# Differential attention scores: two rounded passes over split keys and queries in place of one zero-padded float32 product

## Chip, cores and metric

The kernel runs on one core of a Trainium2 chip. The metric is the device time of one execution in microseconds (us), as the median of the runs shown.

## The reference

Two layers of a trunk over 256 context and 256 latent tokens of width 1024. Three groups of heads work on the same normalised input, side by side: differential attention (group A), latent-compressed attention (group B, "MLA" in the code) and a recurrent scan (group C). A projection, and then a gated feed-forward part, follow. The change touches group A alone: four heads, each with two maps of scores of 64 dimensions.

```python
def diff_attn(q1, q2, k1, k2, v, lam):
    scale = A_DIM ** -0.5
    p1 = softmax32(jnp.einsum('bqhd,bkhd->bhqk', q1, k1) * scale)
    p2 = softmax32(jnp.einsum('bqhd,bkhd->bhqk', q2, k2) * scale)
    a = (p1 - lam * p2).astype(v.dtype)
    return jnp.einsum('bhqk,bkhe->bqhe', a, v)
```

Context queries see the 256 context keys, latent queries all 512. Latent queries and keys are turned by a rotary embedding first. Layer 0 needs both streams, layer 1 the latent queries alone, but the keys of both.

## The kernel before

Every tile has 128 partitions. Queries and keys are held with features on partitions and tokens along the free dimension, so one head's two maps fill the 128 rows: map 1 in rows 0 to 63, map 2 in rows 64 to 127.

Large products run as three rounded passes (`mm3`, L275 to L277): both operands are split into a rounded part and the rest, in the type `F32R` (`fp32r` in the rows), and high x high, high x low and low x high are summed in PSUM. `wgroup` splits each weight tile, rounding on ScalarE (L267) and subtracting on VectorE (L268).

The score product of the differential heads does not use this. `diff_project` makes a head's projection into a PSUM bank of the pool `g`, which has two; `diff_keys` and `diff_query` call it. Its context half is copied by ScalarE (L1070), its latent half goes through `rope` on VectorE (a shuffle at L874, two products, a sum at L882). The query is written twice, into the halves of a tile `qz` that GpSimd has filled with zeros elsewhere (`diff_queries`, L1059 and L1060): one half has map 1's rows and zeros under them, the other the reverse. With this one float32 product over all 128 rows at L1096 gives one map's scores, for 128 queries and 256 or 512 keys. Each product is two records in the trace.

What follows a score: VectorE takes the maximum of each row (L887, in `expsm`), ScalarE the exponential (L888), VectorE combines both maps (L1102), TensorE transposes (L895) and multiplies with the values (L899, in `pv`), ScalarE copies between these.

The work is written as a plan, a string of letters: `q2` projects keys and queries of head 2, `c2` and `l2` are that head's context and latent scores, `x` and `y` MLA heads, `a` a piece of the modulation's projection (L320), `s` steps of the recurrent scan, `v` the values. A scheduler then sets each engine's own order at build time, so instructions of several steps interleave, and engines run their rows strictly in that order. The recurrent part's triangular solver (L688, L690 on VectorE) runs beside the heads.

In layer 0 the weight loads of the output projection wait for the first score product of the last latent head (`late`, passed to `then`).

## Time and profile before

| | us |
|---|---|
| median of 3 runs | 1380.76 (1376.9 to 1381.56) |
| profiled execution | 1380.92 |
| its span | 1379.1 |
| TensorE busy in the span | 1316.6 |
| VectorE busy | 969.1 |
| ScalarE busy | 703.4 |

The span runs from the first to the last instruction. A matmul's record ends when its result is out, so records of successive matmuls overlap, and the step from start to start is what one costs in a row of them. The attention of layer 0 lies at some 240 to 375 us, that of layer 1 at 1037 to 1150.

### The profile page before, as it was taken

The numbers are of one execution on the slowest core, as the hardware profiler recorded it, in microseconds if no ns is written. First come the engines' busy times: TensorE is split into PE (matmuls) and PEld (weight loads), VectorE is DVE, ScalarE is ACT, GpSimd is POOL, SyncE is SP. The second block draws the span as 40 slices with busy tenths as digits, with TensorE's granted clock in tenths as the row PEclk, the third lists the DMA queues.
The fourth block names the chain that finished last, engine by engine and source line by source line (L and its number), as shares of the span: only waits on it lengthen the run. The fifth ranks groups of instructions, "written<-read, shape, count | busy, mean of one in ns | idle before, by whom it ended". The sixth has DMA issues, their size and how long they took to land.

```text
span 1379.1 us, 25815 instructions
## 1 busy us (share of the span) xinstructions
PE 1316.6 (95%) x10184; PEld 1058.2 (77%) x10184; DVE 969.1 (70%) x2430; ACT 703.4 (51%) x1375; POOL 21.1 (2%) x41
## 2 busy tenths in 40 slices
PE   6999999999899999999999999999998998899997
PEld 2687756476666888999998878889874765899996
DVE  3546756685784768866667689668769677867776
ACT  4425343666655454543445654646634654555543
POOL 0001000000000000000000000000100000000000
PEclk9999999999889999999999999999999999999998
DMA  9921342501566747433367436447220029866622
GB/s 317 272 66 47 108 142 95 178 1 62 184 201 211 220 147 232 152 108 107 92 194 262 138 126 196 136 133 222 77 62 1 2 83 315 230 184 187 188 78 84
DMA packets 213162, 201.38 MB, mean 146 GB/s; under 512 B 6528, under 2 KB 168832, under 8 KB 213040
## 3 DMA queue, kind: packets, MB, share of 16 engines
q1 hardware_dynamic: 213040, 199.72, 46.7%
q8 instruction: 80, 1.31, 0.4%
q14 instruction: 42, 0.34, 0.1%
HBM read 197.57 MB, written 2.13 MB: 145 GB/s over the span
## 4 chain that ended last, share of the span: by engine, by line
PE 80%; DVE 12%; ACT 3%; DMA 3%; issue 2%; SPq 0%; DVEq 0%; ACTq 0%
PE g L275 11%; PE g L276 10%; PE g L277 10%; PE acc L275 6%; PE acc L277 6%; PE acc L276 6%; PE r L275 3%; PE r L276 3%; PE r L277 3%; PE acc L320 2%; PE acc L899 2%; PE g L1096 2%; DMA wrm<-in_w_in_dram 1%; PE acc L895 1%; PE g L320 1%
## 5 line engine op out<-in xcount | busy, mean ns | idle before, releaser
L268 DVE TENSOR_TENSOR wlf<-wrf,whf 128x1024 fp32r<-128x1024 f32 x176 | 214.0, 1220 | 41.7 <-ACT whf L267 31.5
L267 ACT ACTIVATE whf<-wrf 128x1024 fp32r<-128x1024 f32 x176 | 183.6, 1050 | 21.8 <-DMA wrf<-in_ffn_w_up_dram 13.4
L275 PE MATMUL g<-hl,whf 128*128 128x256 f32 x528 | 149.3, 285 | 1.3 <-DVE gv L454 1.3
L276 PE MATMUL g<-hl,whf 128*128 128x256 f32 x528 | 148.8, 284 | 0.2 <-DVE hl L413 0.2
L450 ACT ACTIVATE gv<-g,pers 128x256 f32<-128x256 f32 x110 | 62.1, 565 | 166.4 <-PE g L277 164.9
L277 PE MATMUL g<-hl,wlf 128*128 128x256 f32 x528 | 146.5, 284 | 0.0
L453 DVE SCALAR_TENSOR_TENSOR gv<-g,pers,gv 128x255 f32<-128x255 f32 x110 | 52.5, 478 | 79.8 <-ACT gv L450 79.8
L275 PEld LDWEIGHTS g<-hl,whf 128*128 128x128 f32 x528 | 100.8, 191 | 4.4 <-issue 2.0
L276 PEld LDWEIGHTS g<-hl,whf 128*128 128x128 f32 x528 | 101.0, 191 | 2.3 <-DVE hl L413 0.4
L275 PE MATMUL g<-hc,whf 128*128 128x256 f32 x352 | 99.9, 285 | 1.6 <-DVE gv L454 1.2
L277 PEld LDWEIGHTS g<-hl,wlf 128*128 128x128 f32 x528 | 99.6, 191 | 1.3 <-DVE wlf L268 0.8
L276 PE MATMUL g<-hc,whf 128*128 128x256 f32 x352 | 100.0, 285 | 0.0
L277 PE MATMUL g<-hc,wlf 128*128 128x256 f32 x352 | 99.3, 283 | 0.0
L268 DVE TENSOR_TENSOR wlm<-wrm,whm 128x1024 fp32r<-128x1024 f32 (+2 forms) x64 | 72.0, 1133 | 23.8 <-ACT whm L267 21.6
L275 PE MATMUL acc<-whf,at 128*128 128x512 f32 x220 | 87.7, 401 | 0.0
L276 PE MATMUL acc<-wlf,at 128*128 128x512 f32 x220 | 87.3, 397 | 0.5 <-DVE wlf L268 0.5
L277 PE MATMUL acc<-whf,at 128*128 128x512 f32 x220 | 86.2, 393 | 0.0
L267 ACT ACTIVATE whm<-wrm 128x1024 fp32r<-128x1024 f32 (+2 forms) x64 | 62.5, 986 | 35.2 <-PE acc L277 19.3
L275 PEld LDWEIGHTS g<-hc,whf 128*128 128x128 f32 x352 | 67.2, 191 | 5.2 <-issue 3.3
L276 PEld LDWEIGHTS g<-hc,whf 128*128 128x128 f32 x352 | 67.3, 191 | 2.8 <-DVE std L224 0.8
L277 PEld LDWEIGHTS g<-hc,wlf 128*128 128x128 f32 x352 | 67.1, 191 | 0.1
L888 ACT ACTIVATE pa<-g,pers 128x512 f32<-128x512 f32 (+1 forms) x72 | 44.2, 615 | 33.4 <-DVE pers L887 29.2
(534 smaller groups left out, 3455.9 us busy)
## 6 DMA issues: line engine op xcount, KB each, us to landing
wrf<-in_ffn_w_up_dram SPq DMA_DIRECT2D x110, 512.0 KB
wra<-in_ada_w_dram SPq DMA_DIRECT2D x80, 512.0 KB
wrf<-in_ffn_w_down_dram SPq DMA_DIRECT2D x66, 512.0 KB
wrm<-in_w_in_dram SPq DMA_DIRECT2D x52, 512.0 KB
wro<-in_w_out_dram SPq DMA_DIRECT2D x24, 512.0 KB
wrs<-in_ada_w_dram SPq DMA_DIRECT2D x16, 512.0 KB
gt<-gate SPq DMA_DIRECT2D x6, 512.0 KB
wrm<-in_w_in_dram SPq DMA_DIRECT2D x8, 352.0 KB
```

The source lines that it names most:

```text
L267: S.activation(h[:, :n], raw[:, :n], AF.Copy)
L268: V.tensor_tensor(lo[:, :n], raw[:, :n], h.bitcast(F32)[:, :n], ALU.subtract)
L275: first = TE.matmul(ps, lh[0], rh[0], start=start, stop=False)
L276: TE.matmul(ps, lh[0], rh[1], start=False, stop=False)
L277: TE.matmul(ps, lh[1], rh[0], start=False, stop=stop)
L320: ins = TE.matmul(ps[q : q + 32, :], ca[:, k, :], ws[k // 2][:, k % 2 * 512 : k % 2 * 512 + 512], start=k < 4, stop=k >= 4)
L450: S.activation(o[:, : n * SQ], ps[:, : n * SQ], AF.Identity, scale=wc, bias=bias)
L453: V.scalar_tensor_tensor(o3[:, :, 1:SQ], p3[:, :, 0 : SQ - 1], wp, o3[:, :, 1:SQ], ALU.mult, ALU.add)
L888: S.activation(pr_[:, :nk], ps[:, :nk], AF.Exp, bias=m, accum_out=sm)
L895: TE.transpose(pt[:, b * P : (b + 1) * P], prob[:, b * P : (b + 1) * P], ident)
L899: TE.matmul(po[:, :width], pT[:, b * P : (b + 1) * P], vtiles[b], start=(b == 0), stop=(b == nb - 1))
L1096: ins = TE.matmul(ps[:, :nk], qT[:, i, qc : qc + P], kT_[:, :nk], start=True, stop=True)
```

## The change

Keys, queries and their product are made differently; nothing else is edited, but all line numbers behind the change move, by -1 ahead of L1053 and by +24 behind `diff_attn`'s product, which becomes L1119.

- Keys: a head's tile `qk` has two halves, one for each map, each over all 128 rows. In the rows of the map itself stands the rounded key, and in the other 64 rows the rest of it (`split_keys`: a copy on ScalarE, L1061, and a subtraction on VectorE, L1062, for each map and stream). Latent keys go from `rope` into a scratch tile first.
- Queries: they are kept once, in float32, unpadded (`qz`). Ahead of a head's scores `split_queries` fills a tile `qs` for the stream: for each map the rounded query in both halves of the rows (two copies, L1100) and the rest in its own half (a subtraction, L1101) over zeros. Two `qs` tiles are used in turn.
- Product: for each map two passes in `F32R` into one PSUM bank. The first gives high x high plus high x low over 128 rows, the second low x high.

```diff
-    BUFS = dict(... sh=3, ... qk=2, qz=4, va=2, ...)
+    BUFS = dict(... sh=3, ... qk=4, qz=2, qs=2, va=2, ...)
...
-    def diff_queries(late):
-
-        qz = [T("qz", [P, 2, 512]) for _ in range(NQZ)]
-        for t in qz:
-            after(G.memset(t[64:128, 0], 0.0), late)
-            after(G.memset(t[0:64, 1], 0.0), late)
-        return qz
...
+    LOW, HIGH = slice(0, 64), slice(64, 128)
+    OWN = (LOW, HIGH)
+
+    def split_keys(k, c0, src):
+        for i, own in enumerate(OWN):
+            S.activation(k[own, i, c0 : c0 + SQ], src[own], AF.Copy)
+            V.tensor_tensor(k[OWN[1 - i], i, c0 : c0 + SQ], src[own], k.bitcast(F32)[own, i, c0 : c0 + SQ], ALU.subtract)
...
     def diff_keys(l, hh, h, k, tag, late=None):
-        return diff_project(l, hh, 512 + h * P, [(slice(0, P), k)], 1.0, tag, late)
+        def lat(ps):
+            t = T("sh", [P, 4, 256])[:, 0]
+            rope([(slice(0, P), t)], ps, slice(0, P), C("cosa"), C("sina"), SWA)
+            split_keys(k, SQ, t)
+
+        return diff_project(l, hh, 512 + h * P, tag, lambda ps: split_keys(k, 0, ps), lat, late)
 
     def diff_query(l, hh, h, q, tag):
 
-        return diff_project(l, hh, h * P, [(slice(0, 64), q[0:64, 0]), (slice(64, 128), q[64:128, 1])], 0.125, tag)
+        return diff_project(l, hh, h * P, tag, lambda ps: S.activation(q[:, 0:SQ], ps, AF.Copy, scale=0.125),
+                            lambda ps: rope([(slice(0, P), q[:, SQ:512])], ps, slice(0, P), C("cosa"), C("sina"), SWA, 0.125))
+
+    def diff_places(late):
+        qs = [T("qs", [P, 4, SQ], F32R) for _ in range(2)]
+        for t in qs:
+            after(G.memset(t.bitcast(F32)[HIGH, 1], 0.0), late)
+            after(G.memset(t.bitcast(F32)[LOW, 3], 0.0), late)
+        return qs
+
+    def split_queries(to, q):
+        for i, own in enumerate(OWN):
+            for r in OWN:
+                S.activation(to[r, 2 * i], q[own], AF.Copy)
+            V.tensor_tensor(to[own, 2 * i + 1], q[own], to.bitcast(F32)[own, 2 * i], ALU.subtract)
...
-        def head(h, kT_, qT):
+        def head(h, kT_, q, to):
             started = None
+            split_queries(to, q[:, s * SQ : (s + 1) * SQ])
...
-                    ins = TE.matmul(ps[:, :nk], qT[:, i, qc : qc + P], kT_[:, :nk], start=True, stop=True)
-                    started = started or ins
+                    for part in range(2):
+                        ins = TE.matmul(ps[:, :nk], to[:, 2 * i + part, oc : oc + P], kT_[:, i, :nk], start=part == 0,
+                                        stop=part == 1)
+                        started = started or ins
...
-                late = diff["cl".index(op)][0](n, *kq[n])
+                late = diff["cl".index(op)][0](n, *kq[n], qs[turns[0] % 2])
+                turns[0] += 1
```

The scheduler places the new instructions. Three places follow, before and after; numbers behind a tile's name tell tiles of one pool apart.

TensorE in layer 0, in the stretch 275 to 300 us of the profile: context scores (`qk`, `qz`) of heads 2 and 1, between transposes and value products (`pa`, `va`, `vb`). Before:

```order
L1096 MATMUL g_2459<-qk_2041,qz_1351 128x256
L1096 MATMUL g_2460<-qk_2041,qz_1351 128x256
L562 MATMUL r_2897<-pers,d_472_2876 128x128
L899 MATMUL acc_2415<-va_658,pa_2397 128x128 x2
L899 MATMUL acc_2415<-va_659,pa_2397 128x128 x2
L895 MATMUL acc_2428<-pers,pa_2422 128x128 x4
L1096 MATMUL g_2480<-qk_2041,qz_1351 128x256
L1096 MATMUL g_2481<-qk_2041,qz_1351 128x256
L562 MATMUL r_2897<-pers,d_472_2876 128x128
L899 MATMUL acc_2434<-vb_336,pa_2422 128x64 x4
```

The same place after:

```order
L1119 MATMUL g_2510<-qk_2049,qs_1350 128x256 x2
L894 MATMUL acc_2454<-pers,pa_2440 128x128 x4
L1119 MATMUL g_2511<-qk_2049,qs_1350 128x256 x2
L1119 MATMUL g_2533<-qk_2049,qs_1350 128x256 x2
L898 MATMUL acc_2460<-va_658,pa_2440 128x128 x2
L898 MATMUL acc_2460<-va_659,pa_2440 128x128 x2
L894 MATMUL acc_2473<-pers,pa_2467 128x128 x4
L1119 MATMUL g_2534<-qk_2049,qs_1350 128x256 x2
L1119 MATMUL g_2562<-qk_1966,qs_1349 128x256 x2
L898 MATMUL acc_2479<-vb_336,pa_2467 128x64 x4
```

The products keep their neighbours; each map's product is now a pair, and the pieces of the recurrent part (L562) have moved to later rows.

VectorE at the start of layer 1's attention: the rotary sum of head 1's query and what follows it, among the solver's rows (`d`), up to the maxima of the first two scores. Before:

```order
L880 SCALAR_TENSOR_TENSOR sh_10953<-g_10928,pers 128x256
L688 TENSOR_TENSOR d_1441_10306<-d_1494_10709,d_1495_10711 128x96
L882 TENSOR_TENSOR qz_10445<-sh_10953 64x256
L690 TENSOR_TENSOR d_1495_10711<-d_1495_10711,d_1441_10306 128x24x4
L882 TENSOR_TENSOR qz_10445<-sh_10953 64x256
L688 TENSOR_TENSOR d_1441_10306<-d_1494_10709,d_1495_10711 128x115
L268 TENSOR_TENSOR wlm_11671<-wrm_11668,whm_11670 128x1024
L690 TENSOR_TENSOR d_1495_10711<-d_1495_10711,d_1441_10306 128x23x5
L887 TENSOR_REDUCE pers<-g_10960 128x1
```

After:

```order
L881 TENSOR_TENSOR qz_10566<-sh_11073 128x256
L687 TENSOR_TENSOR d_1449_10422<-d_1502_10824,d_1503_10826 128x115
L267 TENSOR_TENSOR wlm_11825<-wrm_11822,whm_11824 128x1024
L689 TENSOR_TENSOR d_1503_10826<-d_1503_10826,d_1449_10422 128x23x5
L1101 TENSOR_TENSOR qs_10560<-qz_10566,qs_10560 64x256
L687 TENSOR_TENSOR d_1449_10422<-d_1502_10824,d_1503_10826 128x110
L1101 TENSOR_TENSOR qs_10560<-qz_10566,qs_10560 64x256
L689 TENSOR_TENSOR d_1503_10826<-d_1503_10826,d_1449_10422 128x22x5
L687 TENSOR_TENSOR d_1449_10422<-d_1502_10824,d_1503_10826 128x126
L886 TENSOR_REDUCE pers<-g_11085 128x1
```

The subtraction that rounds a weight tile (`wlm`), which stood between the query's sums and the first maximum, now stands ahead of the query's two subtractions; the first maximum comes after these and two solver rows more. Two subtractions of the keys (L1062) stand further ahead of this piece.

ScalarE at the same place: the rounding of weight tiles (`whm`), and the exponentials of the first two scores. Before:

```order
L669 ACTIVATE d_1491_10672<-r_10674 128x8x64
L267 ACTIVATE whm_11405<-wrm_11403 128x1024
L267 ACTIVATE whm_11670<-wrm_11668 128x1024
L888 ACTIVATE pa_10959,pers<-g_10960,pers 128x512
L888 ACTIVATE pa_10959,pers<-g_10961,pers 128x512
```

After:

```order
L266 ACTIVATE whm_11550<-wrm_11548 128x1024
L1061 ACTIVATE qk_7396<-sh_11032 64x256 x2
L266 ACTIVATE whm_11824<-wrm_11822 128x1024
L1100 ACTIVATE qs_10560<-qz_10566 64x256 x4
L887 ACTIVATE pa_11084,pers<-g_11085,pers 128x512
L887 ACTIVATE pa_11084,pers<-g_11086,pers 128x512
```

Two copies of the keys and four of the query now stand ahead of the first exponential.

## Rows read from the trace of the kernel before

**Rows 1.** The page's first part: span, and busy time of each engine.
```profile
span 1379.1 us, 25815 instructions
PE 1316.6 (95%) x10184; PEld 1058.2 (77%) x10184; DVE 969.1 (70%) x2430; ACT 703.4 (51%) x1375; POOL 21.1 (2%) x41
```

**Rows 2.** Stretches: length, busy PE, PEld, DVE, ACT, POOL, granted clock, DMA.
```profile
240.00:345.00 105.00, 102.92 (x680) 64.97 (x678) 71.87 (x224) 67.33 (x200) 0.53 (x1) 1.00 0.25 85
275.00:300.00 25.00, 24.51 (x153) 17.78 (x153) 22.34 (x76) 20.07 (x67) 0.00 (x0) 1.00 0.01 2
345.00:375.00 30.00, 25.91 (x156) 17.55 (x157) 24.69 (x78) 21.43 (x52) 0.00 (x0) 0.83 0.51 178
1037.00:1064.00 27.00, 20.46 (x82) 11.08 (x81) 25.59 (x86) 12.98 (x39) 0.00 (x0) 0.87 0.00 1
1064.00:1131.00 67.00, 66.25 (x772) 49.50 (x770) 47.35 (x174) 39.19 (x103) 1.04 (x2) 1.00 0.03 9
1131.00:1150.00 19.00, 15.43 (x84) 11.11 (x84) 13.04 (x28) 13.69 (x25) 0.00 (x0) 1.00 1.03 365
```

**Rows 3.** Groups by line and form, L1096: busy us, mean ns, idle before.
```profile
L1096 PE MATMUL g<-qk,qz 128*128 128x512 f32 x64 | 35.9, 677 | 5.1 <-DVE qz L882 5.1
L1096 PE MATMUL g<-qk,qz 128*128 128x256 f32 x32 | 9.1, 393 | 0.0
...
L1096 PEld LDWEIGHTS g<-qk,qz 128*128 128x128 f32 x96 | 17.1, 206 | 16.9 <-issue 14.5 <-ACT d L529 0.8 <-PE acc L895 0.5
```

**Rows 4.** The same stretches, L1096 alone: busy PE, PEld, clock, DMA.
```profile
240.00:345.00 105.00, 19.08 (x52) 8.45 (x52) 1.00 0.25 85
...
345.00:375.00 30.00, 7.81 (x12) 2.45 (x12) 0.83 0.51 178
1037.00:1064.00 27.00, 10.22 (x16) 3.67 (x16) 0.87 0.00 1
1064.00:1131.00 67.00, 5.91 (x12) 1.96 (x12) 1.00 0.03 9
```

**Rows 5.** The chain that ended last: start us, us, step (xcount: records).
```profile
283.33 0.87 PE g L1096 x4
...
349.93 3.71 PE g L1096 x4
...
1107.35 1.72 PE g L1096 x4
...
1137.21 0.23 PE g L275
```

**Rows 6.** Timeline, rounded matmuls and a weight load: start us, us, instruction.
```profile
1036.50 0.28 PE L277 MATMUL g<-hl,wlm 128*128 128x256 f32 x1
1036.62 0.28 PE L275 MATMUL g<-hl,whm 128*128 128x256 f32 x1
...
370.60 0.63 PE L276 MATMUL acc<-wlo,otc 128*128 128x512 f32 x1
371.03 0.63 PE L277 MATMUL acc<-who,otc 128*128 128x512 f32 x1
...
1036.50 0.19 PEld L275 LDWEIGHTS g<-hl,whm 128*128 128x128 f32 x1
```

**Rows 7.** Groups by line and form: small copies of ScalarE, sums of VectorE.
```profile
L1070 ACT ACTIVATE qz<-g 64x256 f32<-64x256 f32 x8 | 3.0, 374 | 11.6 <-PE g L277 11.6
L1105 ACT ACTIVATE pa<-oh 128x128 f32<-128x128 f32 x24 | 7.5, 312 | 0.4
...
L882 DVE TENSOR_TENSOR qz<-sh 64x256 f32<-64x256 f32 x16 | 6.6, 416 | 0.2
```

**Rows 8.** Timeline of TensorE at layer 1's first scores, with idle before and releaser.
```profile
1042.55 7.15 PE L1096 MATMUL g<-qk,qz 128*128 128x512 f32 x10 [5.05 <-DVE qz L882]
```

**Rows 9.** Timeline of VectorE there: the first two maxima.
```profile
1044.63 0.69 DVE L887 TENSOR_REDUCE pers<-g 128x1 f32<-128x512 f32 x1
...
1046.34 0.69 DVE L887 TENSOR_REDUCE pers<-g 128x1 f32<-128x512 f32 x1 [0.83 <-PE g L1096]
```

More of the change, by code (lines that the diff above doesn't have):

```diff
@@ L101, in nm @@
         return f"{s}_{uid[0]}"
-    BUFS = dict(h=8, hc=4, hl=4, otc=4, otl=4, wrs=13, wrm=3, whm=3, wlm=4, wro=4, who=5, wlo=3, wra=4, wrf=3, whf=4, wlf=6, at=4, al=4, c4=12, d4=12, rk=4, xsc=2, xsd=2, xn=2, nf=5, xs=4, ar=3, gv=3, pa=8, oh=2, sh=3, ob=1, stc=3, std=1, xt=4, gt=2, qk=2, qz=4, va=2, bm=3, lx=1, wx=1, vb=1, bq=3, pc=4)
+    BUFS = dict(h=8, hc=4, hl=4, otc=4, otl=4, wrs=13, wrm=3, whm=3, wlm=4, wro=4, who=5, wlo=3, wra=4, wrf=3, whf=4, wlf=6, at=4, al=4, c4=12, d4=12, rk=4, xsc=2, xsd=2, xn=2, nf=5, xs=4, ar=3, gv=3, pa=8, oh=2, sh=3, ob=1, stc=3, std=1, xt=4, gt=2, qk=4, qz=2, qs=2, va=2, bm=3, lx=1, wx=1, vb=1, bq=3, pc=4)
     def T(tag, shape, dt=F32, pool=None):
@@ L152, in tile_trunk @@
     WO = (0, 2, 3, 1)
-    NQZ = 4
     NBQ = 2
@@ L1053, in diff_v, with diff_project @@
         return ins
-    def diff_queries(late):
-        qz = [T("qz", [P, 2, 512]) for _ in range(NQZ)]
-        for t in qz:
-            after(G.memset(t[64:128, 0], 0.0), late)
-            after(G.memset(t[0:64, 1], 0.0), late)
-        return qz
-    def diff_project(l, hh, c0, to, scale, tag, late=None):
+    LOW, HIGH = slice(0, 64), slice(64, 128)
[4 more added lines that the diff above has]
+            V.tensor_tensor(k[OWN[1 - i], i, c0 : c0 + SQ], src[own], k.bitcast(F32)[own, i, c0 : c0 + SQ], ALU.subtract)
+    def diff_project(l, hh, c0, tag, ctx, lat, late=None):
         wg = wgroup(A["w_in"][l][:, c0 : c0 + P].rearrange("(k p) c -> p k c", p=P), KT, P)
@@ L1068, in diff_project @@
         if hh.first == 0:
-            for r, t in to:
-                S.activation(t[:, 0:SQ], ps[r, 0:SQ], AF.Copy, scale=scale)
+            ctx(ps[:, 0:SQ])
         if hh.last == 512:
-            rope([(r, t[:, SQ:512]) for r, t in to], ps[:, SQ:512], slice(0, P), C("cosa"), C("sina"), SWA, scale)
+            lat(ps[:, SQ:512])
         return ins
     def diff_keys(l, hh, h, k, tag, late=None):
-        return diff_project(l, hh, 512 + h * P, [(slice(0, P), k)], 1.0, tag, late)
-    def diff_query(l, hh, h, q, tag):
-        return diff_project(l, hh, h * P, [(slice(0, 64), q[0:64, 0]), (slice(64, 128), q[64:128, 1])], 0.125, tag)
+        def lat(ps):
[3 more added lines that the diff above has]
+        return diff_project(l, hh, 512 + h * P, tag, lambda ps: split_keys(k, 0, ps), lat, late)
+    def diff_query(l, hh, h, q, tag):
+        return diff_project(l, hh, h * P, tag, lambda ps: S.activation(q[:, 0:SQ], ps, AF.Copy, scale=0.125),
[11 more added lines that the diff above has]
+            V.tensor_tensor(to[own, 2 * i + 1], q[own], to.bitcast(F32)[own, 2 * i], ALU.subtract)
     def diff_attn(l, vt, lam, s, oT, tag):
@@ L1378, in attention @@
         last = [None]
-        kq, qz, diff, late = {}, [], {}, None
+        kq, qn, qs, turns, diff, late = {}, [], [], [0], {}, None
         js = range(0 if hb.joint else 2, 4)
@@ L1398, in attention @@
             elif op == "q":
-                if not qz:
-                    qz.extend(diff_queries(last[0] if QG else Db["start"]))
-                if len(kps) <= n // 2:
-                    kps.append(T("qk", [P, 2, 512]))
-                kq[n] = kps[n // 2][:, n % 2], qz[n % NQZ]
+                if not qs:
+                    qs.extend(diff_places(last[0] if QG else Db["start"]))
+                if len(kps) <= n:
+                    kps.append(T("qk", [P, 2, 512], F32R))
+                if len(qn) <= n // 2:
+                    qn.append(T("qz", [P, 2, 512]))
+                kq[n] = kps[n], qn[n // 2][:, n % 2]
                 diff_keys(l, hboth if hboth and n >= 4 - KD else hb, n, kq[n][0], "g")
@@ L1499, in context1 @@
             yield
-            diff_keys(1, hb, h, kps[h // 2][:, h % 2], "r")
+            diff_keys(1, hb, h, kps[h], "r")
     hc = normed(1, CTX, pcs, ssq, 0, "pre", "hc", ("r",))
@@ L1507, in tile_trunk @@
     va = [T("va", [P, 2, 512]) for _ in range(2)]
-    kps = [T("qk", [P, 2, 512]) for _ in range(2)]
+    kps = [T("qk", [P, 2, 512], F32R) for _ in range(4)]
     side = Side(context1(), phase)
@@ L1517, in tile_trunk @@
     for h in range(max(4 - KD - NGATE, 0), 4 - KD):
-        diff_keys(1, Both(streams=(hc, None)), h, kps[h // 2][:, h % 2], "r", marks[-GATE])
+        diff_keys(1, Both(streams=(hc, None)), h, kps[h], "r", marks[-GATE])
     hl = normed(1, LAT, pcs, ssq, 0, "pre", "hl", ("g", "r"), EC)
```

## The prediction

> **What bounds the kernel now.** I read the page's first part, then the busy time by stretch, then the score products' own rows, and last the chain where those products stand. The profiled execution took 1380.9 us, the span is 1379.1, so 1.8 lie around it; the median of the runs shown is 1380.76, so the sum below is made on 1380.9 and needs no shift. TensorE is busy 95% of the span, VectorE 70%, ScalarE 51% [rows 1]. An average says little here, since the scores exist in two short stages only. Six stretches matter [rows 2]:
> - 240 to 345 us (layer 0; scores of both streams): TensorE 102.92 of 105, VectorE 71.87, ScalarE 67.33. TensorE sets the pace. Inside it lies 275 to 300, where VectorE too is busy 22.34 of 25.
> - 345 to 375 (end of layer 0's attention): TensorE 25.91 of 30 at granted clock 0.83, VectorE 24.69: a chain that passes from one engine to the other.
> - 1037 to 1064 (start of layer 1's attention): VectorE 25.59 of 27, TensorE only 20.46. VectorE sets the pace.
> - 1064 to 1131: TensorE 66.25 of 67.
> - 1131 to 1150 (end of layer 1's attention): 15.43 of 19, a chain again.
>
> The score products at L1096 are 96 records for 48 products, two records each: 32 products of 512 columns, 16 of 256 [rows 3]. By stretch, in records, they number 52, 12, 16 and 12 [rows 4], and the last stretch has the 4 that are left. All 32 records of 256 columns lie in the first stretch (layer 0's context heads), so it holds 16 products of 256 and 10 of 512, and the others hold 6, 8, 6 and 2 of 512.
>
> **What a product costs, before and after.** Busy times of single matmuls overlap, so I take steps in the chain. A float32 product of 512 columns takes 1.72 us for two, so 0.86; of 256 columns 0.87 for two, so 0.43; at half clock 3.71 for two, so 1.86 [rows 5]. The rounded kind stands in the same trace: of 512 columns 0.23 a step [rows 5], of 256 columns 0.12 from start to start (1036.50 to 1036.62), and 0.43 for 512 at half clock (370.60 to 371.03) [rows 6]. Two rounded passes are thus 0.46 and 0.24, and 0.86 at half clock. Saved per product: 0.40 at 512, 0.19 at 256, 1.0 at half clock. The lower bound of the new price is these steps; the upper is the rounded matmul with its 0.19 weight load [rows 6] laid bare each time, 2 x (0.23 + 0.19) = 0.84 and 2 x (0.12 + 0.19) = 0.62, so no saving at 512 and a loss at 256. I take the steps, because in rows 6 the loads of 0.19 already fit into steps of 0.12.
>
> **What is added.** ScalarE: keys had one copy per head and layer for the context, now two, and two more for the latents (+24 over 8 heads); the context query has one copy instead of two in layer 0 (-4); the split query takes four copies for each head and stream, 12 in all (+48). In all +68. Nearest rows: 0.374 us for 64x256 from PSUM, and 0.312 for 128x128 from SBUF [rows 7], so 0.31 to 0.37 and somewhat more; with 0.37 that is 25 us of ScalarE. VectorE: four subtractions per head for keys (+32), two per head and stream for queries (+24), and one rotary sum instead of two (-8): +48. A sum of 64x256 takes 0.416 [rows 7]: 48 x 0.42 = 20 us.
> GpSimd has half the zero fills, and none was waited for; that is nothing. What covers the 20 and 25 us is slack on engines that wait: in 240 to 345 VectorE has 33 us free and ScalarE 38. Without this cover they are paid in full, the rival below.
>
> **The sum, by stretch.**
> - 240 to 345: 16 x 0.19 + 10 x 0.40 = 7.0 off TensorE. Of it, the eight context products of 275 to 300 give 1.5, but there VectorE has 2.7 us free, and the two streams split there bring 4 x 0.42 = 1.7 to it and 8 x 0.37 = 3.0 to ScalarE (20.07 of 25). The order of the changed kernel puts the same c2 and c1 products there. I take nothing for those: **-5.5**.
> - 345 to 375: two products at half clock 2 x 1.0, four at 0.40: 3.6; the chain passes through VectorE and ScalarE as often as through TensorE, so half: **-1.8**.
> - 1037 to 1064: TensorE waits 5.05 us for the query's rotary sum, then runs ten records in 7.15, the first of them at half clock [rows 8]. The order shows four subtractions more (two of the keys, two of the query), one sum less, and the rounding of a weight tile (L268) moved ahead of the query's subtractions. So the first scores are ready later: the first maximum moves from 1044.63 [rows 9] by 4 x 0.42 and a solver row of 0.27 to about 1046.6; but its successors no longer wait for 1.86 us products. VectorE's idle of 0.83 before the second maximum goes, 3 x 0.42 = 1.26 come: **+0.4**, with the product's saving of nothing.
> - 1064 to 1131: 6 x 0.40, full, since TensorE sets the pace: **-2.4**.
> - 1131 to 1150: 2 x 0.40, half: **-0.4**.
>
> Together -9.7. Against it stands what no row shows: a stream's first score now waits for two copies and a subtraction behind the query, 2 x 0.37 + 0.42 = 1.2 at least, 4 x 0.37 + 0.42 = 1.9 at most. There are 12 such places. TensorE runs in order, so behind a waiting score everything waits, also the transposes of the head before, which VectorE and ScalarE wait for in turn. Bounds: none exposed, 0; all, 23 us. In both TensorE stretches the order puts other products between a query and its score, and some splits, head 0's of layer 0 among them, stand long before their use, so I take 2 of 12, 3 us with the wait at its end. -9.7 + 3 = -6.7: **1374 us**. The downstream weight loads of the output projection are released by the last head's first score, so they move with it and take nothing back.
>
> **Rivals.**
>
> *All of it is saved* (chance 0.14). No split is exposed and the shared stretches give their full share: 7.0 + 3.6 + 2.4 + 0.8, and in 1037 to 1064 half of the 4 us that its products shrink: 16, so 1365. For it: splits of the first heads are placed early. Against: VectorE at 95% in one of the stretches.
>
> *Nothing moves* (0.22). TensorE's relief is taken by VectorE and ScalarE, which in these stages were close behind; 20 and 25 us more work fills the slack unevenly, and half of the 12 places expose 1.5: 9 us against 9.7. Then 1380. Another way to it, from the rows: both kernels load 96 weight tiles for the scores (96 records before, mean 206 ns [rows 3]), and if the loads bound the products nothing changes. Against: the steps of 0.12 in rows 6. The Trainium skill (Perfetto Trace Analysis, Identifying the Most-Contended Engine) has the rule that goes with it: matmul busy time misleads, judge TensorE by its weight loads. By it TensorE is only 77% busy [rows 1], and this change relieves it of nothing, 1381.
>
> *Slower* (0.16). The wait in front of each head's first score. At 1.9 us each it eats the 9.7 from the sixth place on, and at 8 of 12 it is 15 us: 1386. TensorE's clock adds to it: in 1037 to 1064, after an idle of 5.05, the granted clock is 0.87, and products run at 1.2 GHz; there the idle grows by about 1.6 us (two key subtractions, 0.84, and two copies, 0.75) while the products that used to fill the time after it shrink, so the half-clock time may go on into the value products. The Trainium skill (TensorE: Matmul & The Clock Gate, Why this matters for your kernels) warns of just that: idle between bursts of matmuls drops the clock. Price: each microsecond of work at half clock loses 0.5, so 2 to 3 us there. For it: ScalarE has to issue four copies in order, behind exponentials. Against: 38 us of free ScalarE in 105.
>
> **The numbers.** The forecast case (0.48) spans 1370 to 1376.5, two exposed places more or less. Since 0.3% (4.1 us) is what a measurement here can tell from no change, faster takes the forecast and the first rival, 0.62; same 0.22; slower 0.16. The range leaves out the deepest saving and the worst of the slower case: 1366 to 1383.
>
> **What would show it.** In the changed trace: score products as pairs that step 0.46 and 0.24; TensorE busy some 15 us less in sum; VectorE up by about 20, ScalarE by 25; 240 to 345 about 5 us shorter to the same point; the wait at layer 1's first score longer than 5.05, near 6.7, with the first maximum some 2 us later and the fourth at the old distance. It would be wrong if waits of TensorE for split queries or keys add up to more than 6 us, or the step of a pair is near 0.8, or TensorE's clock is still at half beyond 1050 us.

## Result and profile after

The changed kernel takes **1412.65 us** (median of 4 runs, 1409.98 to 1415.23); the kernel before took 1378.83 beside it (4 runs, 1376.34 to 1381.56). The ratio is 1.0245, with a 95% interval of 1.0214 to 1.0276: 34 us slower, where 7 us faster were forecast and 1383 was the upper end of the range.

The page's first part, after; it answers to [rows 1]:

```profile
span 1411.5 us, 25899 instructions
PE 1328.4 (94%) x10184; PEld 1073.6 (76%) x10184; DVE 990.9 (70%) x2478; ACT 732.6 (52%) x1443; POOL 14.3 (1%) x33
```

VectorE has 21.8 us more work and ScalarE 29.2, near the forecast 20 and 25. TensorE has 11.8 us more where 15 less were forecast, and its mean granted clock fell from 0.980 to 0.964.

The score products and the copies and subtractions that feed them, from the groups by line and form, after; the first two rows answer to [rows 3]:

```profile
L1119 PE MATMUL g<-qk,qs 128*128 128x512 f32 x64 | 26.4, 509 | 7.0 <-ACT qs L1100 6.9
L1119 PE MATMUL g<-qk,qs 128*128 128x256 f32 x32 | 7.4, 335 | 0.0
L1100 ACT ACTIVATE qs<-qz 64x256 fp32r<-64x256 f32 x48 | 19.9, 414 | 6.0 <-DVE qz L881 3.9 <-PE g L1119 1.3
L1101 DVE TENSOR_TENSOR qs<-qz,qs 64x256 fp32r<-64x256 f32 x24 | 10.0, 415 | 0.8 <-ACT qs L1100 0.4
```

Busy time of the products fell by 11.2 us in sum (45.0 to 33.8). A copy of a query takes 0.414, more than the 0.37 that was assumed, which is half of the excess on ScalarE (48 times 0.044, 2.1 of 4.2 us).

Stretches after, each cut where the same work as in a stretch before begins and ends (columns as in [rows 2]):

```profile
247.00:360.00 113.00, 103.69 (x657) 66.34 (x656) 78.89 (x242) 79.25 (x231) 0.00 (x0) 0.98 0.23 76
402.00:460.00 58.00, 50.44 (x376) 32.17 (x375) 40.86 (x140) 25.23 (x50) 1.57 (x3) 0.82 0.69 220
950.00:980.00 30.00, 25.87 (x197) 24.81 (x196) 26.12 (x72) 20.14 (x37) 0.00 (x0) 0.94 0.74 197
1063.00:1090.00 27.00, 16.24 (x82) 11.55 (x82) 25.52 (x85) 16.21 (x43) 0.00 (x0) 0.87 0.00 1
1090.00:1161.00 71.00, 68.05 (x771) 51.90 (x769) 49.99 (x184) 44.02 (x115) 1.04 (x2) 0.95 0.03 8
```

The second and third answer to these stretches before, which the prediction had not looked at, since no score stands there:

```profile
394.00:441.00 47.00, 45.55 (x470) 30.20 (x468) 26.41 (x83) 27.54 (x60) 1.04 (x2) 0.89 0.72 226
930.00:955.00 25.00, 24.39 (x196) 23.33 (x194) 22.27 (x64) 18.21 (x33) 0.00 (x0) 1.00 0.87 244
```

The stretch that was 240 to 345 is not 5 us shorter but 8 longer: TensorE idles 9.3 us in it, where it idled 2.1. The one behind layer 0's attention is 11 us longer, the one ahead of layer 1's 5, at a lower clock in both.

To add this up without the order of instructions in it, I weighed each matmul of the kernel before that is no score product by its step to the next, and read from each trace when the same sum of work had begun (a worked-out reading from one execution of each kernel; executions of one kernel differ by up to 6 us in all). How much each kernel fell behind the kernel before, by stretches of the kernel before, in us:

| | to 140 | to 240 | to 375 | to 500 | to 930 | to 960 | to 1064 | to 1190 | sum |
|---|---|---|---|---|---|---|---|---|---|
| after | 1.3 | 5.4 | 2.7 | 9.8 | 1.0 | 4.7 | 1.8 | 5.7 | 32.3 |
| e3: split keys and queries, one float32 product | 0.3 | 5.0 | 0.9 | -3.5 | -0.8 | 6.0 | 1.5 | 10.4 | 19.9 |
| e4: padded as before, one rounded pass | -0.9 | 0.0 | -3.0 | 7.2 | -0.7 | 0.0 | 2.7 | 1.0 | 6.3 |
| e6: after, each pass twice | 0.6 | 7.8 | 5.5 | 1.5 | -0.5 | 5.0 | 6.0 | 10.2 | 36.2 |
| e7: padded as before, four rounded passes | -0.5 | 0.0 | 2.5 | 3.8 | 0.8 | 0.0 | 0.2 | 12.8 | 19.7 |
| e5: after, both copies of a key first | 0.5 | 5.4 | 1.6 | 6.3 | -0.7 | 5.2 | 0.3 | 5.7 | 24.3 |
| e16: after, scan's solver earlier | -1.0 | 5.1 | -0.9 | 3.6 | -1.8 | 5.8 | 2.7 | 2.9 | 16.4 |
| e17: the last two edits, and layer 1's keys later | -0.1 | 5.5 | 0.2 | 2.0 | -1.6 | 2.0 | 2.6 | 2.9 | 13.4 |

The scores are in layer 0 up to 375 and in layer 1 from 1037. Of the 32.3 us, 22.2 (1.3, 5.4, 9.8, 1.0 and 4.7) were lost where no score is computed. In e3, which has the split without the shorter product, it is 7.0 of 19.9; there the largest loss, 10.4, lies in layer 1's attention.

### The profile page after: what moved, and what is told of

Same layout as the page of the kernel before. It is cut to its first block, busy times and chain, and to the rows that moved or that the text cites. A ratio compares the mean times of both kernels' runs of the same rounds, so it can differ in the third digit from the quotient of the medians.

```text
span 1411.5 us, 25899 instructions
## 1 busy us (share of the span) xinstructions
PE 1328.4 (94%) x10184; PEld 1073.6 (76%) x10184; DVE 990.9 (70%) x2478; ACT 732.6 (52%) x1443; POOL 14.3 (1%) x33
## 4 chain that ended last, share of the span: by engine, by line
PE 79%; DVE 13%; ACT 4%; DMA 2%; issue 2%; SPq 0%; ACTq 0%; DVEq 0%
PE g L274 11%; PE g L275 10%; PE g L276 10%; PE acc L275 6%; PE acc L274 6%; PE acc L276 6%; PE acc L898 3%; PE acc L319 2%; PE r L274 2%; PE r L276 2%; PE r L275 2%; PE g L1119 1%; PE acc L894 1%; DVE wlm L267 1%; DMA wra<-in_ada_w_dram 1%
## 5 line engine op out<-in xcount | busy, mean ns | idle before, releaser
L886 DVE TENSOR_REDUCE pers<-g 128x1 f32<-128x512 f32 (+1 forms) x72 | 42.2, 595 | 22.3 <-PE g L1119 16.2
```

The lines of the kernel that those rows point to most:

```text
L886: V.tensor_reduce(m, ps[:, :nk], axis=AX.X, op=ALU.max, negate=True)
```

## The experiments

Four readings stand together here for all kernels: the median and its ratio to the kernel before; then, in the profiled execution, the time in score products (from the first record of each unbroken run of them to the start of the next other matmul, less TensorE's idle time in between), TensorE's idle time, and its time at 1.2 GHz. The profiled execution lies up to 6 us from the median (e18: 1387.98). In nine of the eighteen (e4, e6, e8, e9, e10, e12, e16, e17, e18) the median lies outside every range that was written ahead of the run.

| | median us | ratio (95%) | score products | idle | at 1.2 GHz |
|---|---|---|---|---|---|
| before | 1378.83 | | 41.5 | 62.5 | 54.8 |
| after | 1412.65 | 1.0245 (1.0214 to 1.0276) | 31.4 | 83.1 | 101.3 |
| e1_before_scan_held | 1378.96 | 1.0003 (0.999 to 1.0017) | 40.8 | 64.6 | 41.2 |
| e2_after_scan_early | 1411.48 | 1.0243 (1.0221 to 1.0265) | 30.7 | 85.2 | 87.7 |
| e3_split_f32_product | 1398.14 | 1.0148 (1.0127 to 1.0169) | 41.3 | 71.6 | 69.9 |
| e4_padded_one_pass | 1387.07 | 1.0065 (1.0044 to 1.0086) | 18.4 | 77.3 | 84.1 |
| e5_copies_first | 1407.21 | 1.019 (1.0157 to 1.0224) | 29.3 | 83.5 | 82.7 |
| e6_passes_twice | 1417.23 | 1.0284 (1.0263 to 1.0305) | 50.5 | 82.1 | 75.2 |
| e7_padded_four_passes | 1399.78 | 1.0161 (1.0137 to 1.0184) | 48.3 | 70.9 | 71.6 |
| e8_keys_split_only | 1401.64 | 1.0171 (1.0148 to 1.0195) | 42.4 | 73.5 | 57.8 |
| e9_queries_split_only | 1399.36 | 1.0162 (1.0139 to 1.0185) | 42.3 | 74.3 | 66.9 |
| e10_key_tile_per_head | 1383.61 | 1.0025 (1.0008 to 1.0042) | 41.5 | 64.7 | 50.2 |
| e11_plan1_swap | 1385.84 | 1.0044 (1.0029 to 1.0059) | 40.1 | 64.9 | 60.5 |
| e12_twice_in_layer0_latents | 1413.75 | 1.0247 (1.0208 to 1.0285) | 38.2 | 82.9 | 77.7 |
| e13_layer1_keys_later | 1407.56 | 1.0199 (1.0161 to 1.0238) | 31.9 | 84.2 | 92.4 |
| e14_keys_later_copies_first | 1403.87 | 1.0181 (1.0147 to 1.0216) | 30.3 | 79.9 | 77.9 |
| e15_all_three | 1402.41 | 1.0161 (1.0131 to 1.0191) | 38.3 | 77.7 | 74.6 |
| e16_after_scan_before_c2 | 1398.65 | 1.0145 (1.0115 to 1.0174) | 29.8 | 80.5 | 70.6 |
| e17_keys_later_copies_first_scan | 1395.71 | 1.0128 (1.0092 to 1.0164) | 29.4 | 79.7 | 67.3 |
| e18_before_scan_before_c2 | 1382.3 | 1.0022 (1.0004 to 1.0039) | 42.1 | 65.9 | 60.6 |

### What the product is worth, and what the split costs

The split stays, and one float32 product takes the place of the two passes:

```diff
-                    for part in range(2):
-                        ins = TE.matmul(ps[:, :nk], to[:, 2 * i + part, oc : oc + P], kT_[:, i, :nk], start=part == 0,
...
+                    ins = TE.matmul(ps[:, :nk], to.bitcast(F32)[:, 2 * i, oc : oc + P], kT_.bitcast(F32)[:, i, :nk], start=True,
...
```

> The changed kernel with all its split work, but each map's product is one float32 product of the rounded query with the split key (the second pass is left out, and with it the low part of the query). By the order, the scan then stays where it was before. Theory direct (split work costs some 33 us gross, of which the cheaper product gives 11 back): about 1412. Theory order (11 of it is the scan's place, which doesn't move here): about 1401. Theory clock (the rest comes from TensorE having less to do between waits, so that its clock falls): 1380 to 1386, since the products are as long as before.

The kernel before, with padded tiles of the rounded type and so one rounded pass per product:

```diff
-        qz = [T("qz", [P, 2, 512]) for _ in range(NQZ)]
+        qz = [T("qz", [P, 2, 512], F32R) for _ in range(NQZ)]
...
-                    kps.append(T("qk", [P, 2, 512]))
+                    kps.append(T("qk", [P, 2, 512], F32R))
```

> The kernel before with padded queries and keys written in the rounded type and one rounded pass per map in place of the float32 product: no split work at all, the low parts are left out. 32 x 0.63 + 16 x 0.31 = 25 us less product on TensorE. By the order, the scan's last part is displaced by 129 to 242 matmuls, half as long as in the changed kernel. Theory direct: the saving is had where TensorE sets the pace, 1360 to 1366. Theory order: 5 to 8 us of it are lost again, 1366 to 1372. Theory clock: half of the saving or more is lost to half clock, 1372 to 1380.

The split, with the order that it brings, costs 19 us, not 3. And the shorter product is worth nothing in the total even at its best: e4 has no added work and 23 us less of products, and is 8 us slower, where all three theories had it at 1380 or less. It wins 3.0 us at 240 to 375 and loses 7.2 at 375 to 500, where the recurrent part stands elsewhere in its order too. Its stretch that answers to 240 to 345, and its waits of TensorE (line; us in total, times, longest):

```profile
240.00:343.00 103.00, 96.14 (x651) 60.91 (x650) 69.47 (x219) 67.39 (x200) 0.53 (x1) 0.98 0.25 83
```

```profile
PE acc L899 <- ACT pa L896: 8.1, 14, 1.0
...
PE acc L895 <- DVE pa L1102: 5.7, 3, 3.0
```

Of 6.8 us that TensorE is relieved of in the stretch, 2.0 come out; the rest is idle time. The waits of the value products for ScalarE's copies (4.4 us before) and of the transposes for VectorE (1.5) take its place.

The next two go the other way, with the passes of the changed kernel written twice, and e4 with each product made four times:

```diff
-                    for part in range(2):
+                    for part in (0, 1, 0, 1):
```

> The changed kernel with both rounded passes of each map done twice, the second time over the first: four passes, 0.92 us at 512 columns where the float32 product took 0.86. Theory relief (a cheaper product opens gaps in front of the transposes and value products, and TensorE falls to half clock more often): the relief is gone, so about 1398, as with the split work and a float32 product; that is some 14 us faster than the changed kernel though TensorE has 22 us more to do. Theory work (TensorE sets the pace where the scores stand, and what was lost is waits of the split work): 1425 to 1435, since the passes are paid on top.

```diff
-                    ins = TE.matmul(ps[:, :nk], qT[:, i, qc : qc + P], kT_[:, :nk], start=True, stop=True)
-                    started = started or ins
+                    for _ in range(4):
+                        ins = TE.matmul(ps[:, :nk], qT[:, i, qc : qc + P], kT_[:, :nk], start=True, stop=True)
+                        started = started or ins
```

> The padded operands in the rounded type again, with no split work, but each map's pass is done four times over (0.92 us at 512 columns, 0.48 at 256) where one pass took 1387. Theory relief: back to the kernel before, 1376 to 1382, although TensorE has 33 us more to do than with one pass. Theory work: 1400 to 1420. By the order of TensorE's row the scan is displaced as in the changed kernel (214 to 238), which cost nothing when it was displaced alone.

19 us more of products cost e6 only 4.6 us against the changed kernel. The total hides two things: in layer 1's attention (960 to 1190 in the table of stretches) 8.9 us more of products cost 8.7, and at 375 to 500 e6 wins 8.3 back. And e7 has 6.8 us more of products than the kernel before, no split, and takes 21 us more; 12.8 of it fall into layer 1's attention. Length alone explains neither.

The two halves of the split by themselves: the keys made as in the change, then the queries, the other operand as before, and a float32 product (the line of the product alone, against the kernel before). In e9 the product mixes both maps' rows, so that its scores are not the reference's.

```diff
-                    ins = TE.matmul(ps[:, :nk], qT[:, i, qc : qc + P], kT_[:, :nk], start=True, stop=True)
+                    ins = TE.matmul(ps[:, :nk], qT[:, i, qc : qc + P], kT_.bitcast(F32)[:, i, :nk], start=True, stop=True)
...
-                    ins = TE.matmul(ps[:, :nk], qT[:, i, qc : qc + P], kT_[:, :nk], start=True, stop=True)
+                    ins = TE.matmul(ps[:, :nk], to.bitcast(F32)[:, 2 * i, oc : oc + P], kT_[:, :nk], start=True, stop=True)
```

> Only the keys are split as in the changed kernel; queries stay padded float32 and the product is one float32 product of a padded query with the split key tile (the low part of the keys falls on the zeros and is left out). Split work as a whole cost 20 us (1398). Theory keys (the subtractions stand in VectorE's row ahead of the latents' normalisation of layer 1, and between solver and scores in layer 0): 1390 to 1394, with most of the 5 to 6 us at 940 to 960. Theory queries (the wait in front of each head's first score costs most): 1380 to 1385.

> Only the queries are split, into the rounded tiles ahead of each head; keys stay float32 and the product is one float32 product of the rounded query with the unsplit key (both maps' rows are multiplied, so the scores are sums over two maps; the low part is left out). Theory queries: 1390 to 1396, with TensorE's wait for the first score of layer 1 at 6.5 to 7 us and longer waits in layer 1's attention. Theory keys: 1380 to 1385. If the two parts add up, this and the run with split keys are together 20 us above the kernel before.

Keys alone cost 23 us and queries alone 21, both together 19 (e3). They do not add up. Each also gives the engines another order, so either may cost as much by that as by its work; no run separates the two. Only the loss at 930 to 960 goes with one of them: 5.8 us with keys alone, 0.0 with queries alone.

### The keys of layer 1, and two engines at one PSUM tile

VectorE's timeline at 930 to 960 of the kernel before, which is here some 20 to 25 us later:

```profile
961.16 0.88 DVE L1062 TENSOR_TENSOR qk<-r,qk 64x256 fp32r<-64x256 f32 x2
...
962.64 0.43 DVE L1062 TENSOR_TENSOR qk<-r,qk 64x256 fp32r<-64x256 f32 x1
...
963.30 0.75 DVE L230 TENSOR_SCALAR xn<-xt,pers 128x1024 f32<-128x1024 f32 x1
...
966.08 0.43 DVE L1062 TENSOR_TENSOR qk<-r,qk 64x256 fp32r<-64x256 f32 x1 [0.45 <-ACT qk L1061]
...
968.86 0.43 DVE L223 CAST hl<-nf 128x512 fp32r<-128x512 f32 x1
```

ScalarE's, at the same place:

```profile
962.07 0.38 ACT L1061 ACTIVATE qk<-r 64x256 fp32r<-64x256 f32 x1 [2.68 <-DVE qk L1062]
...
965.67 0.38 ACT L1061 ACTIVATE qk<-r 64x256 fp32r<-64x256 f32 x1 [1.74 <-DVE qk L1062]
```

And TensorE's, which waits there for the normalised input:

```profile
969.35 0.58 PE L274 MATMUL g<-hl,whm 128*128 128x256 f32 x1 [3.93 <-DVE hl L223]
```

Seven of the eight subtractions of the context keys stand in VectorE's row ahead of the first tile of layer 1's normalised input (L223, at 968.86), for which TensorE now waits 3.93 us; before it was 0.26. Besides, ScalarE copies map 1, VectorE subtracts map 1 from the same PSUM tile, and only then does ScalarE copy map 2: a wait of 7.3 us in sum, although the two touch different rows. Two kernels take one of these away each: both copies first, then both subtractions (e5); and layer 1's context keys copied to a float32 tile `kc` and split from there when the latent half is (e13). e14 has both.

```diff
+        for i, own in enumerate(OWN):
+            S.activation(k[own, i, c0 : c0 + SQ], src[own], AF.Copy)
         for i, own in enumerate(OWN):
-            S.activation(k[own, i, c0 : c0 + SQ], src[own], AF.Copy)
             V.tensor_tensor(k[OWN[1 - i], i, c0 : c0 + SQ], src[own], k.bitcast(F32)[own, i, c0 : c0 + SQ], ALU.subtract)
```

> The changed kernel with the two rounding copies of a key ahead of its two subtractions, where the changed kernel has copy, subtraction, copy, subtraction on one PSUM bank and the second copy waits for the first subtraction (2.7 us once, at 962). Theory work: the hand-overs between ScalarE and VectorE are halved, 1406 to 1410, with 1 to 2 us less at 950 to 970. Theory order: 1405 to 1420, either way, decided by where the scheduler then puts the scan (183 to 238 matmuls back, as in the changed kernel).

```diff
+            if l:
+                split_keys(k, 0, kc[0][:, h])
             split_keys(k, SQ, t)
...
+        def ctx(ps):
+            if l:
+                S.activation(kc[0][:, h], ps, AF.Copy)
+            else:
+                split_keys(k, 0, ps)
```

> The changed kernel, but layer 1's context keys are copied to a float32 tile as they come and split only when the head's latent keys are. The eight subtractions leave VectorE's row between closing the latents' residual and their normalisation. If they are what costs 4.7 us between 930 and 960: TensorE's wait for the first normalised tile (3.93 us) goes back to 0.3, and 1406 to 1409, unless layer 1's attention, where the split work goes, pays it again (then 1411 to 1414). If it is not them: nothing moves at 930 to 960.

> Both edits to the keys' split together: layer 1's context keys split later, and both copies ahead of both subtractions. If they add up (5.5 and 5 us): 1401 to 1404. If what copies first won was the scheduler's order only: 1406 to 1412.

The medians fall by 5 us with each and by 9 with both; each interval still touches that of the changed kernel (1.0214 to 1.0276), so the size is uncertain. In e5 ScalarE no longer waits for subtractions of one PSUM tile, but the gain is not at 930 to 960 (5.2 lost against 4.7); the largest part of it is at 375 to 500 (6.3 against 9.8), where the order moved as well (next section). In e13 the scheduler left six of the eight subtractions ahead of the normalised input; what went is the hand-over between the engines, TensorE's wait fell to 1.77 us (0.3 was expected), and the loss there fell to 2.0.

### The place of the recurrent scan

The longest loss, 9.8 us, lies at 375 to 500, where the latent scan of layer 0 is solved. Its transposes on VectorE stood at 352.65 us in the kernel before and move behind the attention; after:

```profile
401.08 2.06 DVE L674 STREAM_TRANSPOSE d<-d 128x1024 f32<-128x1024 f32 x1 [0.53 <-PE acc L276]
```

Behind them TensorE meets a load of the modulation's weights that it never waited for at this place:

```profile
414.04 1.05 PE L319 MATMUL acc<-wra,pers 128*32 128x512 f32 x4 [1.33 <-DMA wra<-in_ada_w_dram]
...
423.98 1.92 PE L319 MATMUL acc<-wra,pers 128*32 128x512 f32 x4 [2.48 <-DMA wra<-in_ada_w_dram]
```

Is the place the cause? In e1 the kernel before has this solver held until the last product of the context's output projection; in e2 the changed kernel's plan has its step `s5` ahead of `c0`.

```diff
-                        TE.matmul(pe3[0:64, ci, pd, :], bk[0:64, 0:64], i0, start=True, stop=True)
+                        first = TE.matmul(pe3[0:64, ci, pd, :], bk[0:64, 0:64], i0, start=True, stop=True)
+                        if l == 0 and c2 == 1 and ci + pr + d == 0:
+                            after(first, done[0])
...
+                done[0] = ins
```

> The kernel before with one thing added: the transposes of the second half of layer 0's latent scan (L664 to L667) wait for the last matmul of the context's output projection. Nothing of the change is in it, but the scan's products stand on TensorE's row behind the same number of other matmuls as in the changed kernel (215 to 243 of them at its solver's end, 35 at its states). Theory order (the displaced scan alone costs the 11 us that the changed kernel loses between 390 and 500 us): 1387 to 1391, TensorE's idle time there some 6 us longer, some 10 us more at half clock. Theory direct (the new copies and subtractions cost it themselves, where they stand): 1379 to 1381, nothing to be seen.

```diff
-    PLAN0 = "... p0 x0 a c0 l0 p1 a l1 y0 c2 c1 y1 ... p3 x3 s5 f c3 ..."
+    PLAN0 = "... p0 x0 a s5 c0 l0 p1 a l1 y0 c2 c1 y1 ... p3 x3 f c3 ..."
```

> The changed kernel with one token of layer 0's plan moved: the five steps of the latent scan stand ahead of c0 in place of behind x3. By the order of TensorE's rows the scan's solver is then back where it stands in the kernel before (0 to 4 matmuls off). Theory order: 1401 to 1405, that is 8 to 11 us less than the changed kernel, all of it won between 390 and 500 us. Theory direct: 1411 to 1414.

Held back alone, the solver costs the kernel before nothing (1.0003). Put far ahead, it wins 6 us at 375 to 500 and loses 9 at 240 to 375. Two kernels ask whether any shift in the order would do as much: the kernel before with one key tile per head (`qk=4`), which moves the scan too, and with two steps of layer 1's plan exchanged.

```diff
-                kq[n] = kps[n // 2][:, n % 2], qz[n % NQZ]
+                kq[n] = kps[n][:, 0], qz[n % NQZ]
...
-    PLAN1 = "... p0 s15 q1 l1 l0 s15 ..."
+    PLAN1 = "... p0 s15 q1 l0 l1 s15 ..."
```

> The kernel before with one part of the change that is no work: each head's keys get a tile of their own (four tiles of the pool qk in place of two shared by pairs of heads). Every instruction and its size stay as they are; only the order that the scheduler gives the engines moves, from the first keys on, and the latent scan of layer 0 goes 215 to 243 matmuls back as in the changed kernel. Theory order (any new order of the rows loses what the plan's letters and waits were tuned to): 1390 to 1400, with more idle time of TensorE at 140 to 300 us and in layer 1's attention. Theory work (the added copies and subtractions, and switches between rounded and float32 matmuls, cost what was lost): 1376 to 1381.

> The kernel before with two letters of layer 1's plan exchanged (l0 ahead of l1), no work changed, and the order moved in layer 1's attention alone. Theory order: 1382 to 1390, all of it between 1042 and 1160 us. Theory work: 1376 to 1381.

They cost 3.5 and 6.1 us: a shift of order is worth some microseconds in this kernel, whatever its reason.

More product only where it may hold the scan back (layer 0's latent heads), without and with the edits of e14:

```diff
-                    for part in range(2):
+                    for part in range(2) if l or s == CTX else (0, 1, 0, 1):
```

> The changed kernel with both passes done twice, but only in layer 0's latent heads: 16 products of 512 columns, 2 x 0.23 us more each, 7.4 us more work for TensorE. TensorE's order up to there is that of the changed kernel. Theory clock (in the tail of layer 0's attention and behind it TensorE has so little to do that it runs at half clock, 34 us between 355 and 450 us): the half-clock time there falls by 10 us or more, and the time is 1405 to 1411, less than the changed kernel in spite of the work. Theory work: 1417 to 1420.

> The three edits together: keys of layer 1 split later, copies ahead of subtractions, passes twice in layer 0's latent heads. Theory clock: 1396 to 1402, below the run without the doubled passes. Theory work: 7 us above that run. Neither theory expects the kernel before (1379) to be reached, since the rest of the split work stays.

6.8 us more of products cost 1.1 us (e12), and 8.0 more gained 1.5 (e15): within the intervals both are nothing.

Last, one step `s5` added ahead of `c2` in the plan: to the changed kernel (e16), to e14 (e17) and to the kernel before (e18).

```diff
-    PLAN0 = "... l1 y0 c2 c1 y1 ..."
+    PLAN0 = "... l1 y0 s5 c2 c1 y1 ..."
```

> The changed kernel with five more steps of the latent scan ahead of c2 in layer 0's plan; the later five stay. By the order the solver stands 10 matmuls back (144 in the changed kernel) and its states 129 (238). Theory place (a solver that is late leaves TensorE thin between 400 and 450 us in a kernel whose heads no longer fill it): the loss between 320 and 500 us falls from 8.8 to 0 to 3, and 1403 to 1407. Theory no order: 1411 to 1414.

> The run with keys later and copies first (1403.9), with the same five steps ahead of c2. Its solver stands 10 back already, so theory place expects only its states' 238 to 129 to matter: 1400 to 1404. Theory no order: 1402 to 1406. The kernel before is not reached by either.

> The kernel before with the same five steps ahead of c2. Here they push the solver back instead (146 matmuls, its states 185). When it was held back by a wait nothing was lost, so 1377 to 1381 if the place matters only where the split is; 1384 or more if a late solver costs in any kernel.

VectorE's transposes in e16:

```profile
366.84 1.99 DVE L674 STREAM_TRANSPOSE d<-d 128x1024 f32<-128x1024 f32 x1
```

The one step gives the changed kernel 14.0 us, more than the theory had allowed, and costs the kernel before 3. The loss at 375 to 500 falls from 9.8 to 3.6, TensorE's waits for the modulation's weights fall from 4.2 to 0.3, and the time at 1.2 GHz falls by 31 us. But the place of the transposes alone does not decide what is lost. From 240 to 500, read as in the table of stretches, the changed kernel loses 12.5 us with them at 401.1, and e16 2.7 with them at 366.8. In e1, e9 and e10 they are as late, at 395.6, 404.9 and 389.8, and nothing is lost (-4.0, 0.3 and -3.7); in e4 and e5 they are early, at 351.5 and 371.2, and 4.2 and 7.9 are lost. In e5 and e14 they moved from 401 to 371 without an edit to the plan, so the gain of these runs cannot be told from that of e16. Shown is that another order of the same instructions is worth 14 us in the changed kernel; which displaced row does it is not. With all three edits it takes 1395.7, the lowest of the changed versions (its interval overlaps that of e16), and still 17 us more than the kernel before.

## Why the prediction was wrong

**The price of a pair.** The prediction took 0.46 and 0.24 from long runs of rounded matmuls, and 0.86 and 0.43 for the float32 product from rows where transposes and value products are the neighbours. TensorE's timeline among three kinds of neighbours, before:

```profile
250.45 1.13 PE L1096 MATMUL g<-qk,qz 128*128 128x256 f32 x4
251.51 0.70 PE L524 MATMUL r<-rk,wx 64*128 64x256 f32 x2
252.13 1.05 PE L320 MATMUL acc<-wra,pers 128*32 128x512 f32 x4
253.12 1.12 PE L1096 MATMUL g<-qk,qz 128*128 128x512 f32 x2
254.17 1.05 PE L320 MATMUL acc<-wra,pers 128*32 128x512 f32 x4
...
258.83 0.39 PE L895 MATMUL acc<-pers,pa 128*128 128x128 f32 x2
259.05 1.88 PE L1096 MATMUL g<-qk,qz 128*128 128x512 f32 x4
260.77 0.55 PE L899 MATMUL acc<-vb,pa 128*128 128x64 f32 x4
```

And after:

```profile
256.90 0.50 PE L1119 MATMUL g<-qk,qs 128*128 128x256 f32 x2
257.33 0.70 PE L523 MATMUL r<-rk,wx 64*128 64x256 f32 x2
...
258.39 1.05 PE L319 MATMUL acc<-wra,pers 128*32 128x512 f32 x4
259.38 0.73 PE L1119 MATMUL g<-qk,qs 128*128 128x512 f32 x2
260.04 0.70 PE L523 MATMUL r<-rk,wx 64*128 64x256 f32 x2
...
263.33 0.41 PE L894 MATMUL acc<-pers,pa 128*128 128x128 f32 x2
263.50 0.71 PE L1119 MATMUL g<-qk,qs 128*128 128x512 f32 x2
264.22 0.66 PE L898 MATMUL acc<-vb,pa 128*128 128x64 f32 x4
```

From start to start, a product of 256 columns beside the recurrent part's products fell from 0.53 (two in 1.06) to 0.43; one of 512 behind the modulation's from 1.05 to 0.66; one of 512 between transposes and value products from 0.86 (two in 1.72) to 0.72. So 0.10, 0.39 and 0.14 were saved, where the prediction took 0.19 and 0.40 throughout. In e6 the modulation's neighbourhood holds a pair and then a run of six:

```profile
269.53 0.72 PE L1119 MATMUL g<-qk,qs 128*128 128x512 f32 x2
270.18 1.05 PE L319 MATMUL acc<-wra,pers 128*32 128x512 f32 x4
271.17 1.66 PE L1119 MATMUL g<-qk,qs 128*128 128x512 f32 x6
272.75 1.02 PE L334 MATMUL acc<-ar,pers 128*2 128x512 f32 x2
```

Two cost 0.65 and six 1.58: 0.23 for each further pass, as forecast, and some 0.19 once for a run. What the 0.19 is, no run shows. It could be the change between float32 and rounded matmuls, or the first pass's weight load of 0.19 [rows 6] laid bare, which is the mechanism of the prediction's upper bound. Against the change of kind as the only reason: the float32 product of the kernel before, with no rounded matmul beside it, takes 0.19 more behind the modulation's products than between transposes. With the time at 1.2 GHz counted half, the 48 products took 37.0 us before and 26.1 after: 10.9 saved, where the prediction's steps make 15.8 at full clock (16 x 0.19 + 32 x 0.40). As run they shrank by 10.1, where the sum's savings make 17.8 (7.0 + 3.6 + 4 + 2.4 + 0.8). The step that failed is the choice of the lower bound: the rows with which the price was read had other neighbours than the products have. It is the smaller failure, at most 8 of the some 40 us between forecast and result.

**"TensorE sets the pace" at 240 to 345.** This failed more. TensorE was busy 98% there, and yet in e4 12.8 us less of products in layer 0 bring 3.0 up to 375, and 10.3 us less in layer 1 bring nothing (3.7 are lost). In e6 10.2 us more of products in layer 0 cost 2.8 up to 375; only layer 1's attention passes more products on in full (8.7 of 8.9). The full share that the sum took from this stretch and from 1064 to 1131 was not to be had; the stretch became 8 us longer, of which the work up to 375 gave back 5. The rival "nothing moves" had that mechanism, and no more than 1380 for it.

**The added work.** Its size was right (21.8 and 29.2 us). "What covers it is slack" was wrong: split keys and queries, with the order that they bring, cost 19 us (e3), where the sum had 3 for two exposed waits. In the changed kernel 22.2 of 32.3 us went where the prediction did not look. Some of TensorE's waits, after (line; us in total, times, longest):

```profile
PE g L1119 <- ACT qs L1100: 6.9, 1, 6.9
...
PE acc L898 <- ACT pa L895: 5.5, 12, 0.7
PE acc L319 <- DMA wra<-in_ada_w_dram: 4.2, 4, 2.5
...
PE g L274 <- DVE hl L223: 3.9, 1, 3.9
...
PE acc L894 <- DVE pa L1126: 3.0, 2, 1.8
```

The wait for a split query, of which the sum feared twelve, grew in the one place where a wait had been, by 1.8 us to 6.9 (forecast 6.7), and the first maximum follows the first score by 2.1 us, as before. (The prediction counted four subtractions for the first maximum and three for the same stretch, where the order has four more and one sum less.) What was late was ahead of layer 0's scores (5 us in all kernels of the table that split both), the normalisation ahead of layer 1 (3.9), and the weights of the modulation behind layer 0.

**The order.** The prediction costed each instruction where the order puts it, and treated the moved pieces of the recurrent part as neutral (ahead of it the text says that they moved to later rows, and no term of the sum has them). The stretch in which they now stand has the largest single loss, 9.8 us, and one step of the plan takes back 14 us in all, 6.2 of them there.

**The clock.** Two of the three conditions for being wrong came true. The waits for split queries add up to 6.9 us, over the 6 that were set, though the one wait behind it was forecast at 6.7. And the clock: layer 1's attention had one stretch at 1.2 GHz (1041.0 to 1047.8), and now has 1067.8 to 1074.6, 1101.9 to 1108.8 and 1166.8 to 1170.2. In the whole execution the time at 1.2 GHz grew from 54.8 to 101.3 us. TensorE was at work for 83.0 of these, against 41.7 before; half of the difference is 20.7. With 20.6 us more of idle time, and 10.9 less of products at full clock, that makes 30.4 against a span longer by 32.4. So the loss is idle time and lower clock, about as much of each; this is an account and not yet the cause of the waits. The slower rival named this mechanism and had the right sign, but priced it at 2 to 3 us and put it in front of each head's first score. The rule cited with it (the Trainium skill, TensorE: Matmul & The Clock Gate, Why this matters for your kernels: idle between bursts drops the clock) agrees with the trace, where the clock falls in the wait of 6.9 us. The other rule cited, to judge TensorE by its weight loads, forecast no change; their busy time rose by 1.5% (1058.2 to 1073.6) and does not show the loss.

**What stays open.** Why ahead of layer 0's scores the same 1020 matmuls take 4.4 us more of TensorE's time (half of it is clock at most). Why keys and queries alone cost as much as both. Why e7, without any split, loses 12.8 us in layer 1's attention. Which of the displaced rows costs the 14 us that e16 takes back. Each edit also changes the scheduler's order, so that split work, order and clock cannot be held apart fully: that the split and its order cost more than the product saves is shown, the share of each is not.

## What to carry to other kernels

Price a replaced matmul, and the one that replaces it, between the neighbours that they have, not in a run of their own kind. A busy share of 98% doesn't make an engine the bound of a stretch: ask which wait appears when it is relieved, best by a kernel that leaves the work out and one that doubles it, both read stretch by stretch, since a total can hide a loss in one behind a gain in another. When a scheduler reorders, look first at the stretches that the diff does not touch, and try the displaced step's place in the plan before judging the change.

## What the runs showed of the hardware that was not expected

A run of rounded passes among float32 matmuls took some 0.19 us once, in addition to 0.23 for each pass of 512 columns. A float32 product of 512 columns took 1.05 behind the modulation's products and 0.86 between transposes and value products, all float32. Four rounded passes took less than twice a pair:

```profile
283.37 1.20 PE L1119 MATMUL g<-qk,qs 128*128 128x512 f32 x4
284.50 1.02 PE L334 MATMUL acc<-ar,pers 128*2 128x512 f32 x2
```

They step 1.13 for two products, 0.57 each. And a fall of TensorE's busy share by one point (95% to 94%) went with nearly twice the time at 1.2 GHz.
